# A hybrid decoder layer on one core: the ring of the weights' low parts begins 64 bytes further on

## The chip, the cores and the metric

The kernel runs on one core of a Trainium2 chip. The metric is the time of one execution on the device, in microseconds (us). A core has a matrix engine (TensorE, PE in the profile; its weight loads are listed apart as PEld), three engines for elementwise work (VectorE or DVE, ScalarE or ACT, GpSimd or POOL) and SyncE (SP), whose queue issues nearly all transfers here. All of them work on one memory on the chip of 128 partitions; a tile takes the same range of bytes in each partition, and "place" below means the byte at which that range begins.

## The reference

One decoder layer over 256 positions of width 2048, float32 in and out:

```python
h = rmsnorm(x, pre_mix_g); proj = h @ w_in               # 2048 x 4368
q_a, k_a, v_a, q_b, k_b, v_b, f_b = split(proj)          # 16 heads of 64 in each group
o_a = sliding_window_attention(q_a, k_a, v_a, sinks)     # window 128, ALiBi, 2 kv heads
o_b = forgetting_attention(q_b, k_b, v_b, log_sigmoid(f_b + b_forget))
mix = concat(rmsnorm(o_a, grp_swa_g), rmsnorm(o_b, grp_fox_g)) @ w_out   # 2048 x 2048
x = x + rmsnorm(mix, post_mix_g)
h = rmsnorm(x, pre_ffn_g); u = causal_dwconv(h @ w_up, conv_w, conv_b)   # 2048 x 11264, width 3
gate, val = split(u)
x = x + rmsnorm((gelu(gate) * val) @ w_down, post_ffn_g) # 5632 x 2048
```

## The kernel before

All large products are made from float32 values that are split in two float32r parts, a high part and the rest, the low part. A product is then three: high times high, high times low, low times high. Activations are kept transposed with both parts side by side: in hT, oT and G, 256 columns (the positions) of high parts are followed by 256 of low parts.

The weights pass once through the core in units of up to 1024 values in each partition (4096 bytes). `w_load` brings a unit from device memory into a tile of the ring raw; the transfers are issued by SP. `w_split` makes the two parts: ScalarE copies raw into a tile of the ring whi, rounding it (L103, or L86 in the form whose halves are issued apart), and VectorE subtracts that from raw and writes the low part into a tile of the ring wlo (L106, or L89). raw, whi and wlo have five tiles each and lie one ring behind the other in the pool wp. `w_parts` hands out the two tiles. Two other kinds of tile can stand for them: in the output projection four units are kept for a second use in a pool of their own (`keep`, pool "hold", also named whi and wlo in the profile), and near the end two units lie in the tile rest.

There are two forms of product, and they use the low parts in two ways:

- `unit_T` (q and k, and the up projection): the weights are the loaded operand, 128 columns (512 bytes of each partition) at a time, and the activations stream past them. For each of a unit's 4 x 2 blocks one multiplication loads whi and streams 512 columns of hT, its high and low parts (L212), and one loads wlo and streams the 256 high columns (L217). The order in a unit is six of L212, eight of L217, two of L212. The first group of gates in the up projection has a form of its own (L830 with wlo, L834 with whi).
- `mm3` (v, the output projection, the down projection): the activations are loaded and the weights stream past them, up to 512 columns: three multiplications at L245, with whi, wlo and again whi as the streamed operand. In v's projection the units are cut in blocks of 384 columns (two in a unit) or 272 columns (three in a unit).

The stages run in this order: q, k and v of the first group, v and the forget gates of the second group, its q and k, with attention work woven in between, the output projection, then twice half of the up projection (with convolution and GELU, `conv`, L799 to L807) and half of the down projection. TensorE's order is written by hand throughout; the other engines' orders are made by the planner except in the output projection's second half and at the end. Attention's probabilities p are transposed at L445, the new residual x_sb at L681, both by loading them and streaming an identity; qh and ql (the parts of a q) are loaded at L410. GpSimd's work beside the up projection is a multiplication by a row (L801).

Places: the pools are const, main, wp, small, and behind them the pools of the stages. Unused tiles called room, which no instruction touches, fill the ends of const and small and a gap among the tiles of the feed-forward part. With them the tiles x, hT and y of main, the rings raw, whi and wlo, and the rings oT and G begin at a multiple of 2048 bytes (wlo at byte 126,976 of the partition). Among the attention's tiles, cq takes 128 bytes, and the rings qh, ql and p behind it begin 128 bytes after a multiple of 2048.

```python
const.tile([P, 120], F32, tag="room", name="room_c")
small.tile([P, 368], F32, tag="room", bufs=1, name="room_s")
```

Of the kernel before, what the change touches and what calls it, by code (L numbers as in the profile page):

```python
# [8 lines left out]
F32 = mybir.dt.float32  # L9
F32R = mybir.dt.float32r  # L10
# [7 lines left out]
P = 128  # L18
# [12 lines left out]
def hybrid_layer(ctx: ExitStack, tc: tile.TileContext, x, pre_mix_g, w_in, b_forget, sinks,  # L31
# [10 lines left out]
    wp = ctx.enter_context(tc.tile_pool(name="wp", bufs=4))  # L42
    small = ctx.enter_context(tc.tile_pool(name="small", bufs=4))
# [18 lines left out]

    UNIT = 1024
    WB = 5

    def w_load(src, a, c, pin=False):
        raw = wp.tile([P, UNIT], F32, tag="raw", bufs=5, name="raw")
        i = sp.dma_start(raw[:, :a * c].rearrange("p (a c) -> p a c", a=a), src)
        if pin:
            tc.keep_in_program_order(i)  # L70
        return raw, a, c

    def w_parts(n, keep=None):

        if keep and keep[0] is None:
            return keep[1]
        where, pre, nb = (keep[0], "h", keep[1]) if keep else (wp, "w", WB)
        return [where.tile([P, UNIT], F32R, tag=pre + x, bufs=nb, name="w" + x)[:, :n]
                for x in ("hi", "lo")]

    def w_high(unit, keep=None):

        raw, a, c = unit
        n = a * c
        hi, lo = w_parts(n, keep)
        act.copy(hi, raw[:, :n])  # L86

        def low():
            dve.tensor_tensor(lo, raw[:, :n], hi.bitcast(F32), op=ALU.subtract)  # L89

        return [x.rearrange("p (a c) -> p a c", a=a) for x in (hi, lo)], low

    def w_split(unit, pin=False, keep=None, begun=None, between=None):

        raw, a, c = unit
        n = a * c
        hi, lo = begun or w_parts(n, keep)
        for i in range(2 if between else 1):
            cs = slice(i * 512, i * 512 + 512) if between else slice(0, n)
            if i:  # L100
                between()
            if not between or i:
                i1 = act.copy(hi[:, cs], raw[:, cs])  # L103
                if pin:
                    tc.keep_in_program_order(i1)
            i2 = dve.tensor_tensor(lo[:, cs], raw[:, cs], hi[:, cs].bitcast(F32), op=ALU.subtract)  # L106
            if pin:
                tc.keep_in_program_order(i2)
        return [x.rearrange("p (a c) -> p a c", a=a) for x in (hi, lo)]

    def w_unit(src, a, c, keep=None):
        return w_split(w_load(src, a, c), keep=keep)

    def w_rows(w, k0, a, c0, c):
        return w[k0 * P:(k0 + a) * P, c0:c0 + c].rearrange("(a p) c -> p a c", p=P)
# [8 lines left out]


    const.tile([P, 120], F32, tag="room", name="room_c")
    small.tile([P, 368], F32, tag="room", bufs=1, name="room_s")

    gpre = const.tile([16, P], F32, tag="gpre", name="gpre")
    act.dma_start(gpre, pre_mix_g.rearrange("o (a p) -> (o a) p", p=P))  # L130
# [120 lines left out]
    with tc.tile_pool(name="mixp", bufs=1) as mp:  # L251
# [10 lines left out]
        def x_part(c, k2s, tag="att"):  # L262
            srcs = []
            for k2 in k2s:
                for j in range(2):
                    if tag == "acc" or j == 0:
                        tb = bank(tag)
                    kt = c * 4 + k2 * 2 + j
                    for t in range(2):
                        pe.transpose(tb[:, j * 256 + t * P:j * 256 + (t + 1) * P],  # L270
                                     x_in[:, t, kt * P:(kt + 1) * P], ident)
                    srcs.append((kt, tb[:, j * 256:(j + 1) * 256]))
            to_T(srcs, 0, 256, 0, True)
# [25 lines left out]


        begun = w_parts(UNIT)
        tc.keep_in_program_order(dve.tensor_copy(begun[0][:, 0:512], head[:, 0:512]))
        x_part(0, (0,), "acc")
        bkv = [bank("att"), bank("att")]
        bq0 = [bank(), bank()]
        for u in range(4):
            if u:
                parts = w_split(first[0][u], True)
            else:
                parts = w_split(first[0][u], True, begun=begun,  # L310
                                between=lambda: x_part(0, (1,), "acc"))
# [5 lines left out]
            parts = w_split(first[1][u], True)  # L317
# [232 lines left out]
        for p0, npair, cols in ((0, 3, 384), (3, 3, 384), (6, 2, 272)):  # L550
# [3 lines left out]
            for k0 in range(0, KT, per):  # L554
                na = min(per, KT - k0)
                hi, lo = w_unit(w_rows(w_in, k0, na, c0, cols), na, cols)
# [207 lines left out]
    with tc.tile_pool(name="ffn", bufs=1) as fp:  # L764
# [90 lines left out]
        for half in range(2):  # L855
# [42 lines left out]
            for n in range(3 + (half == 0)):  # L898
                b2 = [bank(), bank()]
                for u in range(FHALF // 2):  # L900
                    hi, lo = w_unit(w_rows(w_down, half * FHALF + u * 2, 2, n * 512, 512), 2, 512)
# [33 lines left out]
        for u in range(FHALF // 2):  # L935
            hi, lo = w_unit(w_rows(w_down, FHALF + u * 2, 2, 1536, 512), 2, 512,
                            keep=(None, [rest[:, c:c + 2, :].rearrange("p a c -> p (a c)")
                                         for c in (4 * (u - LAST), 4 * (u - LAST) + 2)])
                            if LAST <= u < FHALF // 2 - 4 else None)
# [56 lines left out]
```

## Time and profile before

| | us |
|---|---|
| median of 3 runs | 1090.24 |
| lowest, highest | 1089.42, 1090.95 |
| the profiled execution | 1090.18 |
| its span, first to last instruction | 1088.3 |

The profile has one execution. Its page gives busy times of each engine, the span in slices, the chain of work that ended last (each step followed back to what released it), and groups of instructions by source line. Other views group the instructions of one line or of one tile (count, then shortest, median and longest duration in ns, first and last start), list instructions in order of time with neighbours of one kind merged (start, time from the first's start to the last's end, engine, line, tiles, count), or give each engine's busy time in a stretch, in the order PE, PEld, DVE, ACT, POOL. The durations of multiplications reach past the start of the next one, since they overlap; how far apart they start says what one costs.

### The profile page before, as it was taken

The numbers are of one execution on the slowest core, as the hardware profiler recorded it, in microseconds if no ns is written. First come the engines' busy times: TensorE is split into PE (matmuls) and PEld (weight loads), VectorE is DVE, ScalarE is ACT, GpSimd is POOL, SyncE is SP. The second block draws the span as 40 slices with busy tenths as digits, with TensorE's granted clock in tenths as the row PEclk, the third lists the DMA queues.
The fourth block names the chain that finished last, engine by engine and source line by source line (L and its number), as shares of the span: only waits on it lengthen the run. The fifth ranks groups of instructions, "written<-read, shape, count | busy, mean of one in ns | idle before, by whom it ended". The sixth has DMA issues, their size and how long they took to land.

```text
span 1088.3 us, 16295 instructions
## 1 busy us (share of the span) xinstructions
PE 1075.0 (99%) x6002; PEld 932.2 (86%) x6002; DVE 739.7 (68%) x1193; ACT 625.7 (57%) x1069; POOL 183.3 (17%) x252
## 2 busy tenths in 40 slices
PE   9999999999999999999999999999999999999996
PEld 7889988887889888888888888888888888888886
DVE  5987877777567876776767544457777677765563
ACT  7766766666556765656656444456565565644450
POOL 3343344332022110101001000001010110101111
PEclk9999999999999999999999999999999999999998
DMA  8645565554872666656565666655665666666552
GB/s 291 196 129 170 174 190 177 153 158 152 284 243 104 213 197 193 191 178 198 186 193 183 199 192 194 197 189 180 189 195 182 192 191 186 184 196 192 193 171 78
DMA packets 164970, 202.88 MB, mean 186 GB/s; under 512 B 6780, under 2 KB 130972, under 8 KB 164380
## 3 DMA queue, kind: packets, MB, share of 16 engines
q1 hardware_dynamic: 164176, 201.27, 58.2%
q8 instruction: 47, 0.77, 0.3%
q10 hardware_dynamic: 716, 0.58, 0.2%
q14 instruction: 31, 0.25, 0.1%
HBM read 199.58 MB, written 2.11 MB: 185 GB/s over the span
## 4 chain that ended last, share of the span: by engine, by line
PE 89%; DVE 4%; ACT 3%; issue 1%; POOL 1%; DMA 1%; SPq 0%; DVEq 0%; POOLq 0%; ACTq 0%
PE bank_acc L245 34%; PE bank_acc L212 20%; PE bank_att L212 14%; PE bank_acc L217 10%; PE bank_att L217 7%; DVE wlo L106 2%; ACT whi L103 1%; POOL scr L377 1%; PE bank_att L410 1%; PE bank_att L454 1%; PE bank_att L445 1%; ACT p L428 1%; DMA x_in<-in_x_dram 1%; PE bank_att L456 0%; DVE hT L691 0%
## 5 line engine op out<-in xcount | busy, mean ns | idle before, releaser
L106 DVE TENSOR_TENSOR wlo<-raw,whi 128x1024 fp32r<-128x1024 f32 (+3 forms) x357 | 452.8, 1271 | 245.9 <-ACT whi L103 244.2
L103 ACT CAST whi<-raw 128x1024 fp32r<-128x1024 f32 (+3 forms) x356 | 368.5, 1037 | 235.9 <-PE bank_acc L245 119.0
L212 PE MATMUL bank_acc<-hT,whi 128*128 128x512 f32 x1120 | 286.7, 393 | 0.0
L212 PEld LDWEIGHTS bank_acc<-hT,whi 128*128 128x128 f32 x1120 | 200.0, 189 | 34.6
L245 PE MATMUL bank_acc<-whi,G 128*128 128x512 f32 (+1 forms) x724 | 214.8, 379 | 0.0
L212 PE MATMUL bank_att<-hT,whi 128*128 128x512 f32 x672 | 170.9, 392 | 0.1
L217 PEld LDWEIGHTS bank_acc<-hT,wlo 128*128 128x128 f32 x1120 | 151.3, 190 | 9.9
L217 PE MATMUL bank_acc<-hT,wlo 128*128 128x256 f32 x1120 | 157.6, 283 | 0.0
L245 PEld LDWEIGHTS bank_acc<-whi,G 128*128 128x128 f32 x724 | 133.8, 188 | 25.7 <-DVE y_sb L892 0.2
L801 POOL TENSOR_TENSOR u<-u,rowf 128x256 f32<-128x256 f32 x88 | 55.4, 651 | 543.3 <-DVE u L800 541.0
L212 PEld LDWEIGHTS bank_att<-hT,whi 128*128 128x128 f32 x672 | 120.7, 189 | 21.7 <-ACT whi L103 0.3
L245 PE MATMUL bank_acc<-wlo,G 128*128 128x512 f32 (+1 forms) x362 | 137.1, 379 | 0.0
L217 PEld LDWEIGHTS bank_att<-hT,wlo 128*128 128x128 f32 x672 | 91.7, 190 | 7.0 <-DVE wlo L106 0.4
L217 PE MATMUL bank_att<-hT,wlo 128*128 128x256 f32 x672 | 94.0, 282 | 0.0
L245 PE MATMUL bank_acc<-whi,oT 128*128 128x512 f32 (+1 forms) x272 | 83.1, 382 | 0.0
L245 PEld LDWEIGHTS bank_acc<-wlo,G 128*128 128x128 f32 x362 | 68.1, 188 | 12.8
L245 PEld LDWEIGHTS bank_acc<-whi,oT 128*128 128x128 f32 x272 | 50.4, 189 | 9.4
L245 PE MATMUL bank_acc<-wlo,oT 128*128 128x512 f32 (+1 forms) x136 | 51.5, 379 | 0.0
L245 PE MATMUL bank_acc<-whi,hT 128*128 128x384 f32 (+1 forms) x192 | 47.5, 323 | 0.0
L428 ACT ACTIVATE p<-p,nm 128x256 f32<-128x256 f32 (+1 forms) x64 | 28.4, 445 | 28.4 <-DVE nm L416 28.4
L377 POOL TENSOR_TENSOR scr<-scr 128x256 f32<-128x256 f32 x26 | 26.8, 1049 | 49.2 <-DVE scr L376 43.3
L799 ACT COPY cs<-bank_acc 128x256 f32<-128x256 f32 x48 | 15.9, 372 | 32.3 <-PE bank_acc L212 32.3
(187 smaller groups left out, 963.9 us busy)
## 6 DMA issues: line engine op xcount, KB each, us to landing
raw<-in_w_up_dram SPq DMA_DIRECT2D x176, 512.0 KB, 3.4
raw<-in_w_down_dram SPq DMA_DIRECT2D x88, 512.0 KB, 4.6
raw<-in_w_in_dram SPq DMA_DIRECT2D x51, 512.0 KB, 3.9
raw<-in_w_out_dram SPq DMA_DIRECT2D x32, 512.0 KB, 4.6
raw<-in_w_in_dram SPq DMA_DIRECT2D x16, 384.0 KB, 3.8
cb<-c_dram SPq DMA_DIRECT2D x8, 256.0 KB, 3.5
x_sb<-in_x_dram SPq DMA_DIRECT2D x2, 1024.0 KB
raw<-in_w_in_dram SPq DMA_DIRECT2D x5, 408.0 KB, 3.3
```

What stands on the lines that cost most here:

```text
L103: i1 = act.copy(hi[:, cs], raw[:, cs])
L106: i2 = dve.tensor_tensor(lo[:, cs], raw[:, cs], hi[:, cs].bitcast(F32), op=ALU.subtract)
L212: pe.matmul(b, hi[:, a, m * P:(m + 1) * P], hT[:, kt, :], start=(kt == 0), stop=(kt == KT - 1))
L217: pe.matmul(b[:, 256:512], lo[:, a, m * P:(m + 1) * P], hT[:, u * 4 + a, 0:256], start=False, stop=False)
L245: pe.matmul(b, a, r[:, cols], start=(first and i == 0), stop=(last and i == 2))
L377: pool.tensor_tensor(dst, dst, row, op=ALU.mult)
L410: pe.matmul(sb[e][:, cs], a[r, t * P:(t + 1) * P], b[r, 0:nk], start=(n == 0), stop=(n == 2))
L428: act.activation(p[:, e, cs], p[:, e, cs], AF.Exp, bias=nm[:, t, e:e + 1], scale=-1.0, accum_out=rs[:, t, e:e + 1])
L445: pe.transpose(pb[:, i * P:(i + 1) * P], p[:, e, c:c + P], ident)
L454: pe.matmul(ov, values(hl, 0), p[:, :, 0:256], start=(n == 0), stop=False)
L799: act.copy(c, b[:, 256:512])
L801: pool.tensor_tensor(u[:, 2:258], u[:, 2:258], rowf, op=ALU.mult)
```

## The change

`w_parts` hands out a high tile and a low tile as before, but at its first call a tile of 16 float32 values (64 bytes in each partition) is made between the two, in the pool wp and under a tag of its own. The ring wlo therefore lies behind raw, whi and those 64 bytes, and begins at byte 127,040. The unused tile in the pool small is 16 values (64 bytes) smaller, so that all behind it stays where it was. The tiles of the kept units and of rest do not move. No instruction is added.

```diff
     WB = 5
+    rooms = []
...
-        where, pre, nb = (keep[0], "h", keep[1]) if keep else (wp, "w", WB)
-        return [where.tile([P, UNIT], F32R, tag=pre + x, bufs=nb, name="w" + x)[:, :n]
-                for x in ("hi", "lo")]
+        if keep:
+            return [keep[0].tile([P, UNIT], F32R, tag="h" + x, bufs=keep[1], name="w" + x)[:, :n]
+                    for x in ("hi", "lo")]
+        parts = [wp.tile([P, UNIT], F32R, tag="whi", bufs=WB, name="whi")[:, :n]]
+        if not rooms:
+            rooms.append(wp.tile([P, 16], F32, tag="room", bufs=1, name="room_w"))
+        return parts + [wp.tile([P, UNIT], F32R, tag="wlo", bufs=WB, name="wlo")[:, :n]]
...
-    small.tile([P, 368], F32, tag="room", bufs=1, name="room_s")
+    small.tile([P, 352], F32, tag="room", bufs=1, name="room_s")
```

## The prediction

> **What bounds the kernel now.** I read the page's head first, then the slices, then the chain of work that ended last, and then the order of time of TensorE alone in two stages, because a change of place alone can only act through how long single instructions take.
>
> ```profile
> span 1088.3 us, 16295 instructions
> PE 1075.0 (99%) x6002; PEld 932.2 (86%) x6002; DVE 739.7 (68%) x1193; ACT 625.7 (57%) x1069; POOL 183.3 (17%) x252
> PEclk9999999999999999999999999999999999999998
> PE 89%; DVE 4%; ACT 3%; issue 1%; POOL 1%; DMA 1%; SPq 0%; DVEq 0%; POOLq 0%; ACTq 0%
> PE bank_acc L245 34%; PE bank_acc L212 20%; PE bank_att L212 14%; PE bank_acc L217 10%; PE bank_att L217 7%; DVE wlo L106 2%; ACT whi L103 1%; POOL scr L377 1%; PE bank_att L410 1%; PE bank_att L454 1%; PE bank_att L445 1%; ACT p L428 1%; DMA x_in<-in_x_dram 1%; PE bank_att L456 0%; DVE hT L691 0%
> ```
>
> The first two lines show TensorE (PE) at work in 1075.0 of 1088.3 us, at full clock. The two chain lines show that 89% of the time that counts is matrix multiplications and that the writing of the low parts by VectorE (DVE wlo L106) is 2%. So what matters is how far apart two multiplications start. The order of time gives that: the difference of two starts, divided by the count at the end of the line.
>
> ```profile
> 460.51 1.12 PE L217 MATMUL bank_att<-hT,wlo 128*128 128x256 f32 x8
> 461.47 2.00 PE L212 MATMUL bank_att<-hT,whi 128*128 128x512 f32 x8
> 463.31 1.12 PE L217 MATMUL bank_att<-hT,wlo 128*128 128x256 f32 x8
> ...
> 699.77 0.62 PE L245 MATMUL bank_acc<-whi,G 128*128 128x512 f32 x2
> ...
> 700.45 0.62 PE L245 MATMUL bank_acc<-whi,G 128*128 128x512 f32 x2
> ```
>
> In the up projection eight L217 multiplications of 256 columns take 461.47 - 460.51 = 0.96 us, 120 ns each; eight of L212 with 512 columns take 463.31 - 461.47 = 1.84 us, 230 ns each. In the down projection three of 512 columns take 700.45 - 699.77 = 0.68 us, 227 ns each. From 120 and 227 ns, one column costs 107 / 256 = 0.418 ns and each multiplication 120 - 107 = 13 ns beside its columns.
>
> **The change, part by part.** In the program before, raw, whi and wlo are rings of five tiles of 4096 bytes per partition, and each ring begins at a multiple of 2048. Now the wlo ring begins 64 bytes later; the 64 bytes come off the unused room in front of the small tiles, so nothing else moves. The new tile is neither written nor read, so no instruction, wait, semaphore or DMA is added or moved, and no queue (SP's and POOL's among them) is passed: zero, with nothing to hide. (The planner that orders DVE, ACT and POOL gets the same instructions; should it order them otherwise, DVE's idle third covers a swap.) What is left is that the instructions that touch the ring touch other bytes. They are of three kinds.
>
> ```profile
> L217 PEld LDWEIGHTS bank_acc<-hT,wlo x1120: 186/192/193, 12.0 to 958.0; 128*128 128x128 f32 x187
> L217 PEld LDWEIGHTS bank_att<-hT,wlo x672: 186/192/192, 6.9 to 935.7; 128*128 128x128 f32 x168
> L245 PE MATMUL bank_acc<-wlo,G x362: 280/389/398, 593.5 to 1079.3; 128*128 128x512 f32 x163, 128*128 128x256 f32 x18
> L106 DVE TENSOR_TENSOR wlo<-raw,whi x357: 442/1225/2321, 6.0 to 1061.2; 128x1024 fp32r<-128x1024 f32 x167, 128x768 fp32r<-128x768 f32 x8, 128x816 fp32r<-128x816 f32 x2, 128x512 fp32r<-128x512 f32 x1
> L245 PE MATMUL bank_acc<-wlo,oT x136: 280/389/628, 242.0 to 341.8; 128*128 128x512 f32 x120, 128*128 128x256 f32 x16
> L245 PE MATMUL bank_acc<-wlo,hT x96: 285/334/346, 74.0 to 130.0; 128*128 128x384 f32 x64, 128*128 128x272 f32 x32
> ```
>
> First, 1120 + 672 = 1792 weight loads of L217 (512 bytes of each partition) begin 64 bytes after a multiple of 512; the fourth and eighth of each tile now run across a multiple of 2048. (L830 has 48 more.) How much dearer a load may become before it shows is read where loads are the limit:
>
> ```profile
> 342.88 0.98 PEld L830 LDWEIGHTS bank_acc<-hT,wlo 128*128 128x128 f32 x8
> L445 PEld LDWEIGHTS bank_att<-ident,p x96: 137/140/143, 51.3 to 274.2; 128*128 128x128 f32 x96
> L681 PEld LDWEIGHTS bank_att<-ident,x_sb x32: 138/140/142, 334.3 to 348.2; 128*128 128x128 f32 x32
> ```
>
> Eight L830 loads in front of short multiplications span 0.98 us; without the last one's 0.192 that is 0.788 / 7 = 113 ns from load to load, against the 120 ns of L217. So 7 ns of a dearer load are covered by the multiplication, and only what is beyond costs. The other two rows compare places: the p ring of the attention begins 128 bytes after a multiple of 2048 (128 bytes of cq lie before it, and the other rings between are whole kilobytes), x_sb at one. Both loads take 140 ns, though some of p's cross a multiple of 2048. That is another kind of load (plain float32) at 128 bytes, not 64, so it is the nearest row and not the thing itself. Upper end: a load dearer by one more fixed step of 13 ns, 113 + 13 - 120 = 6 ns seen, 1792 x 6 = 10.8 us. Lower end: with all 7 ns won, 1792 x 7 = 12.5 us less. I take 0, as between p and x_sb.
>
> Second, the streamed operand: 362 + 136 + 96 = 594 multiplications of L245 stream a low part. 24 of these read the four units kept in another pool (4 units x 2 rows of weights x 3 multiplications), so 570 begin at other bytes, and one of 512 columns, which is 2048 bytes, now crosses a multiple of 2048. Streams at such places stand in the trace already. In the stage of v's projection a unit is cut into blocks of 384 columns, at bytes 0 and 1536 of the tile (the second crosses 2048), or of 272 columns, at bytes 0, 1088 (17 x 64, so 64 bytes after a multiple of 128) and 2176.
>
> ```profile
> 88.73 0.33 PE L245 MATMUL bank_acc<-wlo,hT 128*128 128x384 f32 x1
> ...
> 89.25 0.33 PE L245 MATMUL bank_acc<-wlo,hT 128*128 128x384 f32 x1
> ...
> 91.85 0.33 PE L245 MATMUL bank_acc<-wlo,hT 128*128 128x384 f32 x1
> ...
> 125.90 0.29 PE L245 MATMUL bank_acc<-wlo,hT 128*128 128x272 f32 x1
> ...
> 126.28 0.29 PE L245 MATMUL bank_acc<-wlo,hT 128*128 128x272 f32 x1
> ...
> 127.41 0.28 PE L245 MATMUL bank_acc<-wlo,hT 128*128 128x272 f32 x1
> ...
> 127.78 0.29 PE L245 MATMUL bank_acc<-wlo,hT 128*128 128x272 f32 x1
> ```
>
> With 384 columns, three multiplications take 0.52 us from 88.73 to 89.25, and 3.12 us for eighteen, 173 ns each, from 88.73 to 91.85, over blocks of both places. With 272 columns three take 0.38 us at byte 1088 (125.90 to 126.28) and 0.37 at 0 (127.41 to 127.78). A start 64 bytes off and a crossing cost at most 0.01 us in three. I take 0. Ends: the fixed 13 ns once more or not at all, 570 x 13 = 7.4 us to either side.
>
> Third, VectorE's 369 writes (357 in the row, 12 of L89), all but the four of the kept units. Their nearest dearer row is one that meets GpSimd:
>
> ```profile
> 580.58 1.23 DVE L106 TENSOR_TENSOR wlo<-raw,whi 128x1024 fp32r<-128x1024 f32 x1 [1.31 <-ACT whi L103]
> 582.92 1.24 POOL L801 TENSOR_TENSOR u<-u,rowf 128x256 f32<-128x256 f32 x2 [9.93 <-DVE u L800]
> 583.66 1.58 DVE L106 TENSOR_TENSOR wlo<-raw,whi 128x1024 fp32r<-128x1024 f32 x1 [0.48 <-ACT whi L103]
> 357.00:593.00 236.00, 235.44 (x1353) 207.07 (x1353) 173.08 (x259) 143.56 (x218) 28.07 (x44) 1.00 0.61 193
> ```
>
> Alone a write takes 1.23 us, beside POOL's 1.58. If every one took 0.35 us more, the 86 of the stage in the last row (the first half of the up projection; its third busy time is DVE's, 173.08 of 236) would add 30 us and still leave DVE idle, and the multiplications would wait only where the chain already goes through DVE wlo: 2% of 1088.3 us is 22 us, times 0.35 / 1.23, 6 us. Lower end 0, since DVE sets nothing else. I take 0: raw, whi and wlo begin alike now, and 1.23 us shows no slowdown that another place could lift.
>
> Sum: 0 + 0 + 0 on a profiled execution of 1090.18 us, of which 1088.3 is span; it lies 0.06 under the median of 1090.24. Forecast 1090.2 us. The ends together: 1090.2 - 12.5 - 7.4 = 1070.3 and 1090.2 + 10.8 + 7.4 + 6 = 1114.4.
>
> A rule that would leave room for more: the Trainium skill, TensorE: Matmul & The Clock Gate, section Back-to-back issue gap, gives N / 2.4 + 2.5 ns between warm multiplications, 109 ns for 256 columns and 216 for 512. The trace has 120 and 227, so 11 ns of each are unexplained by it; were they the price of place, and the new place free of it, an estimate by that page for 570 streams is 6 us less. No row here shows a place with less.
>
> **The rivals.** *Reads of the ring become dearer* (slower). One mechanism: the loads and streams of the ring pay one more fixed step for a start off 2048. It decides from 7 ns per load on, or 4 ns per stream (2.2 us / 570). For it: no float32r load at 64 bytes stands in the trace, the 7 ns of cover are thin, and TensorE has no idle time to give. Against it: p against x_sb, and byte 1088 against byte 0. Time: 1090.2 + 10.8 + 7.4 = 1108.4 in full, half of it, 1099, if only one kind pays.
>
> *The write becomes dearer* (slower): 1096 us by the third term. For it: DVE is where the chain leaves TensorE most often; against it: the slack above.
>
> *Reads become cheaper* (faster): the three rings all begin alike, so a load and a stream that start together may meet at the same place in the memory, and the shift parts them. The 230 ns of L212 against L245's 227 could be such meetings: 8 x 3 ns in each unit of 8 + 8, and 1792 / 8 = 224 units, 5.4 us, so 1085. Against it: L245, whose operands begin alike too, does not show them.
>
> The Trainium skill, SBUF — State Buffer, section Who interferes with whom, has only the port pair of VectorE and GpSimd contend, and TensorE wait for no one; by it the meetings and the dearer write fall away and the time stays. The 1.58 us beside POOL agrees; places are not spoken of there.
>
> **How the numbers follow.** About 0.2%, 2.2 us, is what a measurement of this kernel can tell from no change. No change 0.46, because both nearest comparisons show none; dearer reads 0.27, since the exact place is unseen and every nanosecond would count; dearer write 0.10; cheaper reads 0.17. So faster 0.17, same 0.46, slower 0.37. The likeliest case has 1088 to 1092.4 as its own range. For 8 in 10 the range takes in the cheaper reads to 1085 and the dearer reads up to one kind in full plus a little, 1101.
>
> **What would show it.** In the changed profile L217 should keep 0.96 us for eight, L245 0.68 us for three, and L106 a median of 1225 ns. L217 at more than 120 ns shows dearer loads; L245 streams of wlo above 227 ns, while those of whi stay, show dearer streams; L106 above 1.3 us and waits of PEld for DVE wlo show the write. The forecast is wrong if a float32r load at 64 bytes behaves unlike a float32 load at 128, or if what was taken from blocks of 272 and 384 columns does not hold for 512.

## The result: 0.32% slower, a gain and a larger loss

The changed kernel takes 1092.99 us (median of 12 runs, 1092.33 to 1094.63) beside 1089.37 us (12 runs of the kernel before, taken with it): a ratio of 1.0032, 95% interval 1.0023 to 1.0040. The profiled execution took 1093.13 us with a span of 1091.3 us, 3.0 us more than before. The prediction said 1090.2 us and "no change" as likeliest; its range held the time, but the time did change.

From the page of the changed kernel: the head, the engines' busy times, TensorE's granted clock and the two lines of the chain that ended last. In the changed file all lines behind `w_parts` stand 6 further down (L212 is L218, L217 is L223, L245 is L251, L106 is L112).

```profile
span 1091.3 us, 16295 instructions
PE 1077.1 (99%) x6002; PEld 928.0 (85%) x6002; DVE 740.7 (68%) x1193; ACT 624.5 (57%) x1069; POOL 186.5 (17%) x252
PEclk9999999999999999999999999999999999999999
PE 87%; DVE 5%; ACT 3%; issue 2%; DMA 1%; POOL 1%; SPq 0%; DVEq 0%; POOLq 0%; ACTq 0%
PE bank_acc L251 33%; PE bank_acc L218 19%; PE bank_att L218 14%; PE bank_acc L223 10%; PE bank_att L223 7%; DVE wlo L112 3%; ACT whi L109 1%; POOL scr L383 1%; PE bank_att L416 1%; ACT p L434 1%; PE bank_att L460 1%; DMA x_in<-in_x_dram 1%; PE bank_att L451 1%; DMA raw<-in_w_down_dram 1%; DVE hT L697 0%
```

The counts of instructions are those of before on every engine, and each engine runs them in the same order. The clock is whole. TensorE is still what everything hangs on, so the 3 us have to be in how far apart multiplications start. The order of time of TensorE in the changed kernel (start, time from the first's start to the last's end, line, tiles, count), first in the up projection, then in the down projection:

```profile
459.72 1.11 PE L223 MATMUL bank_att<-hT,wlo 128*128 128x256 f32 x8
460.66 2.00 PE L218 MATMUL bank_att<-hT,whi 128*128 128x512 f32 x8
462.50 1.11 PE L223 MATMUL bank_att<-hT,wlo 128*128 128x256 f32 x8
...
640.04 0.40 PE L251 MATMUL bank_acc<-wlo,G 128*128 128x512 f32 x1
...
643.52 0.40 PE L251 MATMUL bank_acc<-wlo,G 128*128 128x512 f32 x1
```

Eight of L223 take 460.66 - 459.72 = 0.94 us, 118 ns each (before: 0.96 us, 120). Eight of L218 keep 1.84 us. Between the two rows of the down projection lie five groups of three: 3.48 / 15 = 232 ns each (before: 0.68 us for three, 227). So loads of the moved ring became cheaper, and the streaming form became dearer.

A stretch of 100 us of the down projection shows the same by count. The columns are busy time and, in brackets, the instructions seen, for PE, PEld, DVE, ACT and POOL, then the granted clock, the DMA share and GB/s. Before:

```profile
600.00:700.00 100.00, 100.00 (x443) 82.77 (x442) 45.72 (x39) 41.73 (x44) 0.00 (x0) 1.00 0.62 195
```

After:

```profile
600.00:700.00 100.00, 100.00 (x433) 80.91 (x432) 44.22 (x37) 41.00 (x42) 0.00 (x0) 1.00 0.64 193
```

Ten multiplications fewer fit into the same 100 us, 2.3%. The groups by form say which of them slowed. Before, and then after (busy time, mean ns of one, idle before):

```profile
L245 PE MATMUL bank_acc<-whi,G 128*128 128x512 f32 x652 | 202.8, 389 | 0.0
...
L245 PE MATMUL bank_acc<-wlo,G 128*128 128x512 f32 x326 | 126.9, 389 | 0.0
```

```profile
L251 PE MATMUL bank_acc<-whi,G 128*128 128x512 f32 x652 | 206.1, 394 | 0.0
...
L251 PE MATMUL bank_acc<-wlo,G 128*128 128x512 f32 x326 | 128.3, 394 | 0.0
```

The multiplications that stream whi, which did not move, became longer by the same 5 ns as those that stream wlo, and the next multiplication starts 232.0 ns behind the one kind and 232.1 behind the other. That speaks against "a read of the new place costs more"; e7_g64 and e9_all64 below decide it.

The instructions that touch the moved ring, in the changed kernel (shortest, median, longest ns):

```profile
L223 PEld LDWEIGHTS bank_acc<-hT,wlo x1120: 186/188/192, 12.3 to 958.2; 128*128 128x128 f32 x187
...
L251 PE MATMUL bank_acc<-wlo,G x362: 278/395/398, 592.0 to 1082.3; 128*128 128x512 f32 x163, 128*128 128x256 f32 x18
L112 DVE TENSOR_TENSOR wlo<-raw,whi x357: 443/1226/2320, 6.4 to 1064.1; 128x1024 fp32r<-128x1024 f32 x167, 128x768 fp32r<-128x768 f32 x8, 128x816 fp32r<-128x816 f32 x2, 128x512 fp32r<-128x512 f32 x1
```

The load's median went from 192 to 188 ns, the stream's from 389 to 395, VectorE's write from 1225 to 1226.

For the sums here and below I took, for each form, the mean of all distances from one start to the next that are under 300 ns, and multiplied the difference to before by the count of before. Some records are missing from each trace, so the counts are a little under the program's.

| form | count | before, ns | after, ns | sum, us |
|---|---|---|---|---|
| loads wlo, streams 256 of hT (L217) | 1807 | 119.9 | 118.4 | -2.6 |
| loads whi, streams 512 of hT (L212) | 1762 | 230.2 | 229.8 | -0.6 |
| `mm3` on G, 512 columns | 978 | 226.9 | 232.0 | +5.0 |
| `mm3` on oT, 512 columns | 348 | 227.3 | 231.6 | +1.5 |

Together +3.3 us, against 3.0 us of span and 3.6 us of the medians. `mm3` in v's projection (384 and 272 columns) stays within 1 ns in the mean. The distances of 300 ns and more, which hold the waits, add up to 23.6 us before and 22.3 after, so no wait was added. Two spans are not to be compared to a tenth of a microsecond: the profile before has a stretch at half clock (250.05 to 253.46 us) that the other has not.

### The profile page after: what moved, and what is told of

It is laid out like the page before. It is cut to its first block, busy times and chain, and to the rows that moved or that the text cites. A ratio compares the mean times of both kernels' runs of the same rounds, so it can differ in the third digit from the quotient of the medians.

```text
span 1091.3 us, 16295 instructions
## 1 busy us (share of the span) xinstructions
PE 1077.1 (99%) x6002; PEld 928.0 (85%) x6002; DVE 740.7 (68%) x1193; ACT 624.5 (57%) x1069; POOL 186.5 (17%) x252
## 4 chain that ended last, share of the span: by engine, by line
PE 87%; DVE 5%; ACT 3%; issue 2%; DMA 1%; POOL 1%; SPq 0%; DVEq 0%; POOLq 0%; ACTq 0%
PE bank_acc L251 33%; PE bank_acc L218 19%; PE bank_att L218 14%; PE bank_acc L223 10%; PE bank_att L223 7%; DVE wlo L112 3%; ACT whi L109 1%; POOL scr L383 1%; PE bank_att L416 1%; ACT p L434 1%; PE bank_att L460 1%; DMA x_in<-in_x_dram 1%; PE bank_att L451 1%; DMA raw<-in_w_down_dram 1%; DVE hT L697 0%
## 5 line engine op out<-in xcount | busy, mean ns | idle before, releaser
L112 DVE TENSOR_TENSOR wlo<-raw,whi 128x1024 fp32r<-128x1024 f32 (+3 forms) x357 | 453.1, 1272 | 247.3 <-ACT whi L109 246.9
L218 PE MATMUL bank_acc<-hT,whi 128*128 128x512 f32 x1120 | 286.4, 393 | 0.0
L218 PEld LDWEIGHTS bank_acc<-hT,whi 128*128 128x128 f32 x1120 | 199.1, 188 | 34.7
L251 PE MATMUL bank_acc<-whi,G 128*128 128x512 f32 (+1 forms) x724 | 218.1, 383 | 0.5 <-DVE y_sb L898 0.5
L218 PE MATMUL bank_att<-hT,whi 128*128 128x512 f32 x672 | 170.6, 392 | 0.1
L251 PEld LDWEIGHTS bank_acc<-whi,G 128*128 128x128 f32 x724 | 133.8, 188 | 29.4 <-DVE y_sb L898 0.7
L223 PEld LDWEIGHTS bank_acc<-hT,wlo 128*128 128x128 f32 x1120 | 150.3, 189 | 9.8
L223 PE MATMUL bank_acc<-hT,wlo 128*128 128x256 f32 x1120 | 155.9, 282 | 0.0
L218 PEld LDWEIGHTS bank_att<-hT,whi 128*128 128x128 f32 x672 | 120.2, 188 | 21.8 <-ACT whi L109 0.3
L251 PE MATMUL bank_acc<-wlo,G 128*128 128x512 f32 (+1 forms) x362 | 138.5, 383 | 0.0
L223 PEld LDWEIGHTS bank_att<-hT,wlo 128*128 128x128 f32 x672 | 91.3, 189 | 6.8 <-DVE wlo L112 0.4
L223 PE MATMUL bank_att<-hT,wlo 128*128 128x256 f32 x672 | 93.2, 281 | 0.0
L251 PE MATMUL bank_acc<-whi,oT 128*128 128x512 f32 (+1 forms) x272 | 83.5, 383 | 0.0
L251 PEld LDWEIGHTS bank_acc<-wlo,G 128*128 128x128 f32 x362 | 67.9, 188 | 14.6
L251 PEld LDWEIGHTS bank_acc<-whi,oT 128*128 128x128 f32 x272 | 50.2, 188 | 10.2
L251 PE MATMUL bank_acc<-wlo,oT 128*128 128x512 f32 (+1 forms) x136 | 51.7, 380 | 0.0
L251 PE MATMUL bank_acc<-whi,hT 128*128 128x384 f32 (+1 forms) x192 | 47.6, 324 | 0.0
```

Of the source, the lines that this page charges most:

```text
L218: pe.matmul(b, hi[:, a, m * P:(m + 1) * P], hT[:, kt, :], start=(kt == 0), stop=(kt == KT - 1))
L223: pe.matmul(b[:, 256:512], lo[:, a, m * P:(m + 1) * P], hT[:, u * 4 + a, 0:256], start=False, stop=False)
L251: pe.matmul(b, a, r[:, cols], start=(first and i == 0), stop=(last and i == 2))
```

## The experiments

"Distance" below is the place of the loaded operand less the place of the streamed one, in bytes and modulo 512. (The loaded blocks begin 512 bytes apart and the streams of 512 columns at one place modulo 2048, so each distance stands for itself and for 512 more; the last section says why these are taken as one. A distance of starts, in ns, is one in time.) Each kernel's time is against the kernel before, run on the same chip.

**A control (e1_slab0).** To move loaded and streamed low parts apart, the five low tiles were made ranges of one long tile, first at the old places.

```diff
+    slab, given = [], [0]
+    LOADED, STREAMED = 0, 0
...
+        if not slab:
+            slab.append(wp.tile([P, WB * UNIT + 16], F32R, tag="wlo", bufs=1, name="wlo"))
+        c = given[0] % WB * UNIT + at
+        given[0] += 1
+        return [hi, slab[0][:, c:c + n]]
```

> The five tiles of the low parts become five ranges of one tile, at the places of the kernel before (loaded and streamed low parts both at multiples of 2048). This is the control for the next two: if the form of the ring is indifferent, 512-column multiplications of the down projection stay 226.9 ns apart, the 256-column ones with loaded low parts 119.9 ns, and the time is that of before within 0.2% (about 1089 us).

1089.94 us, ratio 1.0006 (0.9996 to 1.0015). `mm3` on G at 226.9 ns, L217's form at 120.0. The form itself costs nothing.

**Only the loaded low parts move (e2_loads64).** The same with

```diff
-    LOADED, STREAMED = 0, 0
+    LOADED, STREAMED = 16, 0
```

> Only the low parts that are loaded (q, k and the up projection) lie 64 bytes on; those that are streamed (v, output and down projection) lie at multiples of 2048. If loads and streams answer to the place each on their own: L217-type multiplications 118.4 ns apart instead of 119.9, the down projection's 226.9 ns as before, time 3 us below before (about 1086.3). If the shift only costs: no gain, 1089.4 or more. If the gain of the loads in the changed kernel came from its streams' delays: 119.9 ns, 1089.4.

1098.14 us, ratio 1.0085 (1.0069 to 1.0102). The distances of the starts are those of the changed kernel for L217's form (118.5 ns, -2.4 us) and for L212's (-0.7 us), and `mm3` stays at 226.9 ns. That part tells that the 2.6 us won come from the loads alone. The time is another matter, and it is my construction: a moved range reaches 64 bytes into the next one, which ties a unit's write and reads to its neighbour's where streamed and loaded units follow each other. VectorE's order is another here: a write of wlo that it does at 232.54 us in the control comes at 244.43, and TensorE waits for its end. At the second long wait TensorE waits for the write of a loaded unit (L98) that reaches into the range it is about to read; there, in two multiplications of this run and of the next, 16 columns of low parts are a neighbour's. The control, which differs in the 64 bytes alone, has neither wait. TensorE in the order of time there (in brackets: idle before, and what ended it):

```profile
241.68 0.39 PE L254 MATMUL bank_acc<-whi,oT 128*128 128x512 f32 x1
245.70 0.80 PE L254 MATMUL bank_acc<-wlo,oT 128*128 128x512 f32 x1 [3.63 <-DVE wlo L115]
246.29 1.05 PE L254 MATMUL bank_acc<-whi,oT 128*128 128x512 f32 x2
247.15 0.63 PE L254 MATMUL bank_acc<-wlo,oT 128*128 128x512 f32 x1
...
326.68 0.61 PE L254 MATMUL bank_acc<-whi,oT 128*128 128x512 f32 x2
331.15 0.79 PE L254 MATMUL bank_acc<-wlo,oT 128*128 128x512 f32 x1 [3.86 <-DVE wlo L98]
...
967.47 0.50 PE L254 MATMUL bank_acc<-wlo,G 128*128 128x512 f32 x1 [0.62 <-DVE wlo L115]
```

From 241.68 to 245.70 nothing starts, and after that two multiplications take 247.15 - 246.29 = 0.86 us, 430 ns each. The stretches behind the two long waits, and behind the short one, by the same columns as above:

```profile
245.70:252.50 6.80, 6.80 (x21) 5.54 (x22) 4.67 (x7) 2.30 (x5) 4.68 (x7) 0.58 0.72 228
...
331.20:338.00 6.80, 6.80 (x19) 5.36 (x20) 0.00 (x0) 0.00 (x0) 0.00 (x0) 0.59 0.25 77
...
967.60:972.00 4.40, 4.40 (x20) 3.63 (x21) 4.01 (x8) 2.57 (x4) 2.22 (x2) 1.00 0.86 278
```

The clock granted is 0.58 and 0.59 for some 7 us after each wait of about 4 us; after the third wait it stays at 1.00. Distances of 300 ns and more add up to 37.6 us here and to 20.3 us in the control, 17.3 us more. Of these, 5.4 us are 24 multiplications on oT that the slow clock moved into this group, and 2.9 us were won beside the control; what is left is 9.0 us, and the spans differ by 8.8 (1096.8 and 1088.0). The Trainium skill, TensorE: Matmul & The Clock Gate, section What's actually happening, says that the clock is at half after at least one idle window of about 3.4 us and at full speed after at least one busy window of that length. The trace agrees in part: idle times of 3.63 and 3.86 us bring a fall, 2.6 and 2.7 us into them, and 0.62 us does not, and each time the clock stood at half for 6.8 us (244.65 to 251.48 and 329.99 to 336.81), in 5.8 and 5.7 us of which TensorE was at work. So long an idle time was not needed in the kernel before: its clock fell at 250.05, and the longest idle time of TensorE in the 6 us ahead of that was 0.94 us.

**Only the streamed low parts move (e3_streams64).** `LOADED, STREAMED = 0, 16`.

> The opposite half: only the streamed low parts lie 64 bytes on. If loads and streams are independent: 119.9 ns for the loaded kind, 232 ns instead of 226.9 in the down projection (990 multiplications, 5.0 us) and 231.6 in the output projection (350, 1.5 us), time 6.5 us above before (about 1095.9).

1094.09 us, ratio 1.0044 (1.0029 to 1.0059). The 100 us of the down projection:

```profile
600.00:700.00 100.00, 100.00 (x433) 80.92 (x432) 44.23 (x37) 41.00 (x42) 0.00 (x0) 1.00 0.61 191
```

433 again, as in the changed kernel; 232.0 ns on G (+5.0 us) and 231.6 on oT (+1.5 us), L217's form at 120.0 as before. So the change is, in the distances, the sum of two effects of opposite sign, one of the loads and one of the streams. The time is 4 to 5 us above before where 6.5 were expected: the distances of 300 ns and more add up to 2.1 us less than in the control (18.2 and 20.3), and the spans differ by 4.4 us (1092.4 and 1088.0). Why they are less is open.

**Twice the step (e4_lo128).** The ring 128 bytes further on instead of 64.

```diff
-            rooms.append(wp.tile([P, 16], F32, tag="room", bufs=1, name="room_w"))
+            rooms.append(wp.tile([P, 32], F32, tag="room", bufs=1, name="room_w"))
...
-    small.tile([P, 352], F32, tag="room", bufs=1, name="room_s")
+    small.tile([P, 336], F32, tag="room", bufs=1, name="room_s")
```

> The low ring begins 128 bytes beyond a multiple of 2048 instead of 64; all else as in the changed kernel. If a stream of 512 columns pays for crossing a multiple of 2048: 232 ns in the down projection as with 64. If what matters is the place within 128 bytes: 226.9 ns and 119.9 ns as before, time 1089.4. If the distance itself matters: other values than both.

1100.11 us, ratio 1.0101 (1.0086 to 1.0116).

```profile
600.00:700.00 100.00, 100.00 (x430) 80.50 (x429) 45.89 (x42) 40.97 (x44) 0.00 (x0) 1.00 0.59 189
```

`mm3` on G at 233.1 ns (+6.1 us), and now L217's form is dearer too, 121.1 ns (+2.2 us). A start at a multiple of 128 is no cure; what matters is not the place within 128 bytes.

**Across 2048 without a small step (e8_lo1024).** The ring 1024 bytes further on (256 values, and 112 in the room behind).

> The low ring begins 1024 bytes beyond a multiple of 2048: a 512-column stream crosses such a multiple in its middle. If crossing costs: 232 ns in the down projection. If the place within 256 or 1024 bytes counts: 226.9 and 119.9 ns, 1089.4 us, with 128 bytes' 233 ns as the contrast.

1089.93 us, ratio 1.000 (0.999 to 1.001), and `mm3` on G at 226.9 ns though now every stream of 512 columns of wlo crosses a multiple of 2048 in its middle:

```profile
600.00:700.00 100.00, 100.00 (x442) 82.78 (x442) 45.29 (x38) 42.17 (x43) 0.00 (x0) 1.00 0.64 195
```

Crossing costs nothing, and 1024 bytes are as good as none.

**Both rings move alike (e5_both64).** The 64 bytes stand before whi, so that whi and wlo both begin 64 bytes beyond a multiple of 2048.

```diff
+        if not rooms:
+            rooms.append(wp.tile([P, 16], F32, tag="room", bufs=1, name="room_w"))
         parts = [wp.tile([P, UNIT], F32R, tag="whi", bufs=WB, name="whi")[:, :n]]
-        if not rooms:
-            rooms.append(wp.tile([P, 16], F32, tag="room", bufs=1, name="room_w"))
```

> The rings of the high and of the low parts both begin 64 bytes beyond a multiple of 2048. If a 512-column stream pays for crossing a multiple of 2048: all three multiplications of a triple in the down and output projections cross now, about 232 to 237 ns each, 6.5 us or more slower there. If the price comes from streams that follow each other at unlike places: all streams of a stage begin alike again, 226.9 ns. The loaded low parts: 118.4 ns as in the changed kernel if load against stream is what matters there; time then 1086 to 1087.

1087.95 us, ratio 0.9984 (0.9974 to 0.9993).

```profile
600.00:700.00 100.00, 100.00 (x438) 82.05 (x437) 44.89 (x37) 41.31 (x43) 0.00 (x0) 1.00 0.63 193
```

L217's form falls to 115.2 ns (-8.4 us), L212's rises to 232.7 (+4.4), `mm3` on G is at 228.9 (+2.0) instead of 232.0, which neither expected case had. So a part of the changed kernel's loss was that its two rings were unlike.

**Only whi moves (e6_hi64).** The two rings change their order, wlo at its multiple and whi behind the 64 bytes.

> The two rings change places, and the high parts begin 64 bytes beyond a multiple of 2048, the low parts at one. If the price comes from streams at unlike places: the down projection takes about 232 ns again, as now two of three streams are off and one is not. If from crossing alone: more than in the changed kernel, since twice as many streams cross. The loaded low parts go back to 119.9 ns if their own place is what matters; the 512-column multiplications with loaded high parts stay 229.7 to 230.2.

1100.23 us, ratio 1.0096 (1.0081 to 1.0112). `mm3` on G at 233.2 ns (+6.2 us), on oT at 232.8 (+1.9), L212's form at 233.1 (+5.2), L217's at 119.1 (-1.5). L212's form was expected to stay; its loaded high parts lie at a distance of 64 now, and it rises as in e5_both64.

**Only the loaded operand of the down projection moves (e7_g64).** All weights at their old places; G and what lies behind it 64 bytes further on.

```diff
-        fp.tile([P, 384], F32, tag="room", name="room_f")
+        fp.tile([P, 400], F32, tag="room", name="room_f")
```

> The rings stay at multiples of 2048; the loaded operand of the down projection (the ring G) begins 64 bytes beyond one. If load against stream decides: the down projection leaves 226.9 ns (about 232 if symmetric), the output projection (whose loads did not move) keeps 227.3. If only streams count: 226.9 ns, time of before, 1089.4.

1095.43 us, ratio 1.0049 (1.0034 to 1.0064). Order of time in the down projection:

```profile
640.15 0.39 PE L245 MATMUL bank_acc<-wlo,G 128*128 128x512 f32 x1
...
643.65 0.40 PE L245 MATMUL bank_acc<-wlo,G 128*128 128x512 f32 x1
```

3.50 / 15 = 233 ns (+6.3 us on G), with no weight moved and every stream alike; on oT, which stayed, 227.4 as before. This tells most: the loss needs neither a stream at another place nor successive streams that are unlike. What load and stream are to each other is enough.

**Everything behind moves along (e9_all64).** As with both rings, but the room in small stays 368 values, so that oT, G and the rest lie 64 bytes further on too. In the output and down projections load and stream begin at like places again; in the q, k and up stages the loads begin 64 bytes beyond hT.

> Both rings and everything behind them (the kept units, oT, G, the attention's tiles) begin 64 bytes later; hT, x, y and raw stay. In mm3 the load and the stream begin at like places again, in the q, k and up stages the load begins 64 bytes further on than hT. If only the place of load against stream counts: mm3 back at 226.9 ns in G and 227.3 in oT, L217 115 ns and L212 232.7 ns as with both rings moved, so -8.4 + 4.4 = -4 us, 1086 us. If a place of its own, 64 bytes beyond a multiple, costs a stream something whatever is loaded: mm3 at 229 to 232 ns, so 2 to 6 us more, 1088 to 1092 us.

1085.01 us, ratio 0.9961 (0.9947 to 0.9974): faster than before.

```profile
460.53 1.07 PE L222 MATMUL bank_att<-hT,wlo 128*128 128x256 f32 x8
461.44 2.02 PE L217 MATMUL bank_att<-hT,whi 128*128 128x512 f32 x8
463.30 1.07 PE L222 MATMUL bank_att<-hT,wlo 128*128 128x256 f32 x8
```

```profile
600.00:700.00 100.00, 100.00 (x443) 82.81 (x442) 44.74 (x38) 42.02 (x43) 0.00 (x0) 1.00 0.63 195
```

In this kernel L222 is the form of L217, and L217 that of L212. Eight of the first take 0.91 us, 114 ns each, eight of the second 1.86 us, 232 ns. The down projection is back at 443 in 100 us, though no tile that is loaded or streamed in this stretch begins at a multiple of 2048 any more.

**The same with 32 and with 96 bytes (e10_all32, e11_all96).** 8 and 24 values in place of 16.

> The same with 32 bytes. If only the place of load against stream counts: mm3 at 226.9 ns whatever the distance; the L217 and L212 multiplications tell whether 32 bytes do in the q, k and up stages what 64 do (115 and 232.7 ns, 1086 us) or nothing (120 and 230 ns, 1090 us). If places of their own count, mm3 moves too.

> The same with 96 bytes. If only the place of load against stream counts: mm3 at 226.9 ns; the L217 and L212 multiplications between those of 64 bytes (115 and 232.7 ns) and of 128 bytes beyond (L217 121 ns), so 1086 to 1092 us. If places of their own count, mm3 moves too.

1093.67 us, ratio 1.0042 (1.0028 to 1.0055), and 1093.54 us, ratio 1.0040 (1.0027 to 1.0054). The down projection with 32 bytes, and then with 96:

```profile
600.00:700.00 100.00, 100.00 (x443) 82.81 (x442) 46.67 (x42) 42.61 (x45) 0.00 (x0) 1.00 0.63 195
```

```profile
600.00:700.00 100.00, 100.00 (x443) 82.84 (x442) 46.84 (x42) 42.45 (x45) 0.00 (x0) 1.00 0.63 195
```

443 at every common place: 226.9 ns on G in all three. What was lost is lost in the q, k and up stages, where the distances are 32 and 96: L212's form at 233.0 and 233.8 ns (+5.0 and +6.4 us), L217's at 119.7 and 118.8 (-0.4 and -2.0 us). Both times are above those expected (1086 or 1090, and 1086 to 1092): L212's form loses as much as at 64 or more, and L217's wins less.

**The other sign (e12_ht64).** hT begins 64 bytes further on, in a tile that is 1024 bytes longer; y, raw, whi and wlo follow 1024 bytes later, and the room in small is 1024 bytes smaller. The later hT (hT2) gets the same edit, and rest begins where it did.

```diff
-    small.tile([P, 368], F32, tag="room", bufs=1, name="room_s")
+    small.tile([P, 112], F32, tag="room", bufs=1, name="room_s")
...
-    hT = main.tile([P, KT, 512], F32R, tag="hT", name="hT")
+    hT = main.tile([P, KT * 512 + 256], F32R, tag="hT", name="hT")[:, 16:8208].rearrange("p (k c) -> p k c", k=KT)
```

> The other sign: in the q, k and up stages the stream hT begins 64 bytes further on and the loaded rings stay (y, raw, whi and wlo go 1024 bytes on, which by the run with 1024 bytes does nothing). If the distance between load and stream counts whatever its sign: L217 115 ns and L212 232.7 ns, mm3 of the output and down projections 227 ns as before, 1085 us as with everything behind moved. If it must be the load that begins further on: L217 stays at 118 to 120 ns while L212 rises to 232 or so, 1090 to 1095 us. In v's projection, where hT is loaded, the 384-column blocks may move by some ns either way (192 multiplications, under 1 us).

1082.16 us, ratio 0.9934 (0.9920 to 0.9947), the fastest of all and below what either theory gave it.

```profile
457.11 1.07 PE L217 MATMUL bank_att<-hT,wlo 128*128 128x256 f32 x8
458.02 1.99 PE L212 MATMUL bank_att<-hT,whi 128*128 128x512 f32 x8
459.85 1.11 PE L217 MATMUL bank_att<-hT,wlo 128*128 128x256 f32 x8
460.79 2.00 PE L212 MATMUL bank_att<-hT,whi 128*128 128x512 f32 x8
462.62 1.07 PE L217 MATMUL bank_att<-hT,wlo 128*128 128x256 f32 x8
```

Eight of L217 take 0.91 us and then 0.94, in turns; eight of L212 1.83 us, 229 ns each. Sums: -5.7 and -1.8 us. So the sign counts: 64 bytes the other way win on the 512-column form instead of losing.

All kernels beside each other. "Up" is the distance in the q, k and up stages for whi and for wlo, "down" that in the output and down projections (for e7_g64 the down projection alone); in ns the mean distance of starts.

| kernel | up: whi, wlo | L212's form | L217's form | down: whi, wlo | `mm3` on G |
|---|---|---|---|---|---|
| before | 0, 0 | 230.2 | 119.9 | 0, 0 | 226.9 |
| e10_all32 | 32, 32 | 233.0 | 119.7 | 0, 0 | 226.9 |
| e9_all64 | 64, 64 | 232.7 | 115.2 | 0, 0 | 226.9 |
| e11_all96 | 96, 96 | 233.8 | 118.8 | 0, 0 | 226.9 |
| e12_ht64 | -64, -64 | 229.2 | 116.7 | 0, 0 | 226.9 |
| e5_both64 | 64, 64 | 232.7 | 115.2 | -64, -64 | 228.9 |
| e7_g64 | 0, 0 | 230.2 | 120.2 | 64, 64 | 233.3 |
| after | 0, 64 | 229.8 | 118.4 | 0, -64 | 232.0 |
| e6_hi64 | 64, 0 | 233.1 | 119.1 | -64, 0 | 233.2 |
| e4_lo128 | 0, 128 | 230.5 | 121.1 | 0, -128 | 233.1 |

## Why the prediction failed, step by step

**What bounds the kernel, and reading it by distances of starts:** right. All 3 us were found as distances, and no wait was involved.

**No instruction, order or queue moves:** right, by equal counts and orders.

**The first term, 1792 loads at 0:** wrong in its size, -2.6 us, within its ends. The failing step is the comparison of p with x_sb. It compared how long loads last, in stages whose streams are short; in the kernel it is the pairing with the stream beside them that counts, and that row does not hold it. The price of a load of its own, the "one more fixed step of 13 ns" of the upper end, which would have put L217's form at 126 ns, was met at no place tried: it is between 115.2 and 121.1 ns in all kernels.

**The second term, 570 streams at 0:** wrong, +6.5 us. It is within the 7.4 us given as an end, but by accident: that end counted only streams of wlo at 13 ns each, and what happened is 5 ns on each of 1326 multiplications, two thirds of them streaming whi. The failing step is the carrying over from blocks of 384 and 272 columns. The sums on those rows were right, and these forms indeed stayed within 1 ns in the changed kernel, but the rows could not stand for the new place. The two places of the 384 columns, 0 and 1536, are 3 x 512 bytes apart, which is one distance, not two. The 272 columns, at 0, 1088 and 2176, do have distances of 0, -64 and -128, but their mean does not answer to distance (127.9 to 128.6 ns in all kernels). A form of 512 columns behaves otherwise. The prediction named this as its weak point ("if what was taken from blocks of 272 and 384 columns does not hold for 512"), and it was.

**The third term, VectorE's write at 0:** right, 1225 and 1226 ns.

**The rivals.** "Reads become dearer" had the sign and not the mechanism: it blamed a start off 2048, and e9_all64 and e12_ht64 are faster with starts off 2048, while e7_g64 is as slow with all weights on it. "The write becomes dearer" did not occur. "Reads become cheaper" came nearest to the mechanism, a load and a stream that start together meeting in the memory, and L217's form does become cheaper with a distance. It failed in its sum, because it took it that any distance helps, and because it turned one row the wrong way. That L245, whose operands begin alike, sits at 227 ns was held against it as a sign of no interaction. It was the sign of a good pairing, which the change gave up. Nor were the 230 ns of L212 a steady price: in the kernel before, with one distance throughout, the eight of L212 in a row start 233, 235, 229, 232, 231, 227, 227 and 227 ns apart (means over all units). They settle at what L245 has, and the 3 ns more are those of the first five.

The Trainium skill was used for a rival's counterweight: SBUF — State Buffer, section Who interferes with whom, by which TensorE waits on no one and its two reads have a port each. The runs disagree in effect: moving only the loaded operand (e7_g64) lengthens the distance from 227 to 233 ns. Whether the two reads meet in the memory or in TensorE's own queue no run shows. Nor does one show which load meets which stream: in the down projection of the kernel before, the load that starts 3 ns after a stream is that of the next multiplication, and the runs do not tell it from the stream's own.

The 11 ns between the Trainium skill's formula (TensorE: Matmul & The Clock Gate, section Back-to-back issue gap, 109 ns for 256 columns) and L217's 120 ns, which the prediction called a possible price of place, are in part one, of the pairing and not of the ring's own place: in e9_all64 the form runs at 113 to 114 ns after the first of each eight. For 512 columns (216 ns) the least seen as a mean is 226.9.

## What to carry to other kernels

Where TensorE is the bound, an operand's place is to be judged with its partner: put the loaded and the streamed operand of each stage at a chosen distance, and let all operands of one sequence of multiplications share that distance (for `mm3`, 0 and -64 mixed cost more than either alone). Measure the distance for each form of multiplication, since the best one differs (here 0 for 512 columns with the activations loaded, -64 or +64 for 256 columns with the weights loaded). And when a neighbouring row is taken as a stand-in, it must have the same pairing and the same length; a row that shows no effect shows it for its own form only.

## What the runs showed that I had not expected

The distances repeat in patterns, and a pattern belongs to the distance, not to the stage or the operand. Successive distances of starts in steady stretches, worked out from the traces:

```
distance   form and kernel            ns from start to start, repeating
0          mm3 on G, before           226 227 227
+64        mm3 on G, e7_g64           231 236
+64        L212's form, e9_all64      231 236
-64        mm3 on G, e5_both64        226 229 232 | 225 230 231
-64        L212's form, e12_ht64      226 229 232 | 225 230 231
0, -64     mm3 on G, after            231 237 240 225 225 230 232 233 230 236 231 229 234 235 232
-64, 0     mm3 on G, e6_hi64          235 228 237
0, -128    mm3 on G, e4_lo128         236 234 230
```

The stage with the activations loaded and the one with the weights loaded show the same pair of numbers at +64 (231, 236) and the same triples at -64. At -64 alone `mm3` has 228.9 ns, at 0 alone 226.9; mixed in one sequence they have 232.0, more than either. Each start seems to depend on the one before, so that unlike neighbours keep the sequence from settling; that fits the rows and is not shown. L217's form at one and the same distance of 64 runs at 118 ns in the changed kernel, where the six multiplications ahead of it have a distance of 0, and at 113 to 114 in e9_all64, where they have 64; in e12_ht64 it takes either value from one unit to the next.

1024 bytes are no distance (e8_lo1024), and 128 are one (e4_lo128). 512 are none either: the loaded blocks of the two halves of the positions begin 512 bytes apart, and `mm3` on G starts every 226 or 227 ns with both in the kernel before, and in turns after 231 and 236 ns with both in e7_g64. So if the period is a power of two, it is 256 or 512 bytes. What in the memory or in TensorE has that period stays open, and so does why 384 and 272 columns barely react in the mean (177.8 to 180.7 and 127.9 to 128.6 ns in all kernels).

A change of allocation alone was worth 7.6 us of 1090: e12_ht64, with hT 64 bytes further on and the tiles behind it 1024, is 0.66% faster than the kernel before (0.53% to 0.80%).
